# Start-up of a diffusion backbone step: products with constants from the start, four shifts on VectorE, a third chunk buffer, and the first normalized activations without GpSimd

## The chip, the core and the metric

The kernel runs on one core of a Trainium2 chip. The metric is the device time of one execution in microseconds (us); lower is better. TensorE (PE in the profile) multiplies matrices, VectorE (DVE) and ScalarE (ACT) do elementwise work, GpSimd (POOL) does slower elementwise work, and SyncE (SP) issues nearly all DMA transfers. Each engine executes its own instructions strictly in the order in which the program lists them, and waits on semaphores for the others.

## The reference

One inference step of a two-layer backbone over 384 tokens (256 latent and 128 context), model width 1024. The start of the program, which the change touches, is this part:

```
sh1, sc1, gt1, sh2, sc2, gt2 = split(silu(c) @ w_mod[l] + b_mod[l], 6)   # for c and for c_ctx
h = rmsnorm(x, norm_g[l, 0]) * (1 + sc1) + sh1                           # c for latents, c_ctx for context
z = h @ w_in_even                                                        # 1024 -> 3584
...                                                                      # attention, retention, output projection
x = x + gt1 * rmsnorm(m, norm_g[l, 1])
h = rmsnorm(x, norm_g[l, 2]) * (1 + sc2) + sh2
x = x + gt2 * rmsnorm(swiglu(h), norm_g[l, 3])
```

w_mod of a layer has 6144 columns, so 24 MB; the modulation of both layers is 48 MB of weights for two vectors c. Layer 0 has neighbourhood attention and retention (the even layer), layer 1 an HGRN2 mixer.

## The kernel before, in words

Everything is transposed: the model width lies on the 128 partitions in eight blocks (KT = 8, index j or k), tokens lie along the free axis (NT = 384). Every large product is made of three f32r products: activations are split into a high part `hh` and a low part `hl`, weights into `wh` (ScalarE) and `wl` (VectorE), and hh*wh + hh*wl + hl*wh is accumulated. A weight tile is 128 x 1024, eight blocks, 512 KB; three raw buffers `wr` and three pairs of split buffers rotate.

The modulation weights come in 48 chunks of 1 MB, in the order of MOD_ORDER. A chunk holds two blocks of 128 columns, for layer 0's first norm shift j and scale j (MOD_CHUNKS). "pe" chunks are multiplied by TensorE (`mod_pe`, eight products of 256 columns, then `mod_pe_out`: a ScalarE copy to `mev` and two small products with `sel` that add the four partial sums and turn them), "dve" chunks by VectorE (`mod_dve`, four multiply-and-accumulate instructions into `mscr`, against c spread over all partitions in `msb`). `mod_finish` adds the bias and makes the scale (1 + sc) * g. Two buffers `mraw` hold chunks.

The first norm (class `Norm`) doesn't wait for the root mean square. Of the first product group E1 (six output blocks, 8 x 6 x 3 = 144 matmuls), k goes over the blocks as they arrive: `early_hi` makes x[k] * scale on ScalarE and appends the two columns of shifts (386 columns), `early_lo` makes the low part on VectorE. The 1/rms row rB comes later and is applied when the six results leave. The other groups (E2, E5: 72 matmuls of 512 columns each, tokens as the stationary side; E3, E4, E6) use the truly normalized h, which `normed` makes per block: t = x * rB on GpSimd, hh = A t + S on ScalarE, the same once more into f on VectorE, hl = f - hh on VectorE. Attention starts with products of ka and qa, two of E1's results.

The order of the instructions is written by a planner (`Machine`): generators yield operations, and at each step the one with the earliest start by the planner's own costs is emitted, ties by priority. Its constants (COLD, the DMA rate in `Build.dma`) set the order on all engines and no more. load_mods interleaves chunk i with x[i]; load_weights the weight tiles; `rest` (line 1626) starts the loads of layer 0's other constants and `mod_dve`.

Of the kernel before, what the change touches and what calls it, by code (L numbers as in the profile page):

```python
# [36 lines left out]
P = 128  # L37
D = 1024
KT = 8
# [38 lines left out]
CB_AT = 4  # L78
# [21 lines left out]
COLD = 16.0  # L100
# [115 lines left out]
class Build:  # L216
# [71 lines left out]
    def dma(self, out, in_):  # L288
# [3 lines left out]
                  [a for a in here if a is in_], n / 355e3)  # L292
# [54 lines left out]
MOD_ORDER = ([("pe", 0, c) for c in range(8)]  # L347
# [9 lines left out]
def pack_mod(w):  # L357
# [120 lines left out]
def emit_all(nc, tc, ctx, io, outs):  # L478
# [24 lines left out]
    acc, rB = sb(cp, "acc", [NT]), sb(cp, "rB", [NT])  # L503
    acc2, rsd = sb(cp, "acc2", [NT]), sb(cp, "rsd", [96])
# [44 lines left out]
    start.loads = 0  # L549

    def load_mods():
        for i, (kind, l, ci) in enumerate(MOD_ORDER):
            r, = yield from mraw.take()
            yield I.dma(r, io["w_mod"][i])
            (mods.pe if kind == "pe" else mods.dve).append((l, ci, r))
            if i < KT:
                yield I.dma(x[:, i], io["xT"][:, i])
                start.loads = i + 1

# [17 lines left out]
    def mod_pe():  # L577

        for l, *chunks in MOD_PE:
# [15 lines left out]
            M.spawn(mod_pe_out(l, chunks, b), -1, margin=M_MOD)  # L595
# [12 lines left out]

    def mod_late():
# [7 lines left out]
    def mod_dve(phase, b):  # L617

        yield lambda: W.used >= DVE_FROM
        yield I.dma(b.sb, io["cB"])  # L620
        yield lambda: phase == 0 or len(W.norm.hs) == KT
        yield I.act(b.sb, b.sb, AF.Silu)
# [18 lines left out]
    mods.n, mods.over, mods.flying, mods.now = 0, set(), 0, False  # L641

# [152 lines left out]
    class Norm:  # L795


        def __init__(self, l, which):
# [9 lines left out]
            for par in range(2):  # L808
                M.spawn(self.normed(par), 2)

        def loads(self):
            for j in range(KT):
                yield lambda: start.loads > j
# [31 lines left out]
        def early_hi(self):  # L845
            for j in range(KT):
                yield lambda: self.x > j and (self.l, 12 * self.which + j) in mods.done
                for who, a, e in HALVES:
                    yield I.act(hh[:, j, a:e], x[:, j, a:e], AF.Identity, scale=self.coef(j, who)[0])
                yield I.act(hh[:, j, NT:NX], mod[self.l][:, 24 * self.which + j])  # L850
# [866 lines left out]
```

## Time and profile before

| | |
|---|---|
| median of 3 runs | 1129.93 us (1129.28 to 1131.42) |
| the profiled execution | 1129.32 us, its span 1127.5 us |
| PE busy | 1088.1 us (97% of the span) |
| DVE busy | 819.9 us (73%) |
| ACT busy | 541.8 us (48%) |
| POOL busy | 136.7 us (12%) |
| first product on PE | 6.87 us |
| first product of E1 | 13.32 us |
| first product of E2 | 52.40 us |
| first product of the first FFN-side output group after the retention norm | 211.94 us |

The profile is one execution. In the timeline a row gives the start, the duration, the engine, the source line, the operation with its output and inputs, how many instructions were merged, and in brackets how long the engine had sat idle before it and on what. Busy times of PE are modelled: consecutive matmuls overlap in the record, so the distance between two starts, not the duration, is what one costs.

### The profile page before, as it was taken

The numbers are of one execution on the slowest core, as the hardware profiler recorded it, in microseconds if no ns is written. First come the engines' busy times: TensorE is split into PE (matmuls) and PEld (weight loads), VectorE is DVE, ScalarE is ACT, GpSimd is POOL, SyncE is SP. The second block draws the span as 40 slices with busy tenths as digits, with TensorE's granted clock in tenths as the row PEclk, the third lists the DMA queues.
The fourth block names the chain that finished last, engine by engine and source line by source line (L and its number), as shares of the span: only waits on it lengthen the run. The fifth ranks groups of instructions, "written<-read, shape, count | busy, mean of one in ns | idle before, by whom it ended". The sixth has DMA issues, their size and how long they took to land.

```text
span 1127.5 us, 18541 instructions
## 1 busy us (share of the span) xinstructions
PE 1088.1 (97%) x7180; PEld 1011.7 (90%) x7180; DVE 819.9 (73%) x1524; ACT 541.8 (48%) x1002; POOL 136.7 (12%) x143
## 2 busy tenths in 40 slices
PE   6999999899999999999999999999999999999996
PEld 5778888679999999999887988888989999999995
DVE  2598888687989999995888489996786444444334
ACT  3585555368333333323765456655666333333321
POOL 1220000000000000234024046352000000000001
PEclk9999999999999999999999999999999999999998
DMA  9966544534667677565341322223224333333431
GB/s 351 359 215 215 168 149 132 215 136 152 233 241 240 238 245 240 205 227 167 135 156 62 127 85 85 76 76 103 94 84 141 122 123 129 123 123 129 131 112 56
DMA packets 49688, 180.44 MB, mean 160 GB/s; under 512 B 6560, under 2 KB 13728, under 8 KB 43072
## 3 DMA queue, kind: packets, MB, share of 16 engines
q1 hardware_dynamic: 49536, 179.18, 46.7%
q8 instruction: 56, 0.92, 0.3%
q14 instruction: 32, 0.26, 0.1%
q0 software_dynamic: 64, 0.08, 0.0%
HBM read 174.79 MB, written 3.41 MB: 158 GB/s over the span
## 4 chain that ended last, share of the span: by engine, by line
PE 77%; DVE 15%; issue 3%; DMA 2%; ACT 1%; SPq 1%; POOL 0%; DVEq 0%; ACTq 0%; POOLq 0%
PE bank L226 76%; DVE wl L252 3%; DVE mscr L265 2%; DMA mraw<-in_w_mod 2%; DVE XB L252 1%; DVE XA L252 1%; SPq L291 1%; DVE TA L252 1%; DVE scr L258 1%; PE bank L230 1%; DVE scr L252 1%; DMA ro<-qk 0%; DVE ZW L252 0%; DVE ac L282 0%; POOL ZW L250 0%
## 5 line engine op out<-in xcount | busy, mean ns | idle before, releaser
L226 PE MATMUL bank<-hh,wh 128*128 128x384 f32 (+1 forms) x1248 | 431.0, 345 | 0.0
L226 PE MATMUL bank<-hh,wl 128*128 128x384 f32 (+1 forms) x1248 | 425.4, 341 | 0.0
L226 PE MATMUL bank<-hl,wh 128*128 128x384 f32 (+1 forms) x1248 | 391.0, 344 | 0.0
L252 DVE TENSOR_TENSOR wl<-wr,wh 128x1024 fp32r<-128x1024 f32 x216 | 272.5, 1262 | 128.2 <-ACT wh L244 128.0
L244 ACT ACTIVATE wh<-wr 128x1024 fp32r<-128x1024 f32 x216 | 228.1, 1057 | 151.2 <-PE bank L226 106.0
L226 PEld LDWEIGHTS bank<-hh,wh 128*128 128x128 f32 x1248 | 237.9, 191 | 6.4 <-ACT scr L244 2.4
L226 PEld LDWEIGHTS bank<-hh,wl 128*128 128x128 f32 x1248 | 237.5, 190 | 0.9 <-issue 0.3
L226 PEld LDWEIGHTS bank<-hl,wh 128*128 128x128 f32 x1248 | 232.4, 189 | 5.6 <-issue 2.0
L265 DVE SCALAR_TENSOR_TENSOR mscr<-mraw,msb 128x1024 bf16<-128x1024 f32 x128 | 159.4, 1245 | 3.5 <-ACT msb L244 2.4
L226 PE MATMUL bank<-gh,wl 128*128 128x384 f32 x352 | 118.2, 336 | 1.8 <-DVE wl L252 1.8
L226 PE MATMUL bank<-gh,wh 128*128 128x384 f32 x352 | 117.6, 334 | 0.0
L226 PE MATMUL bank<-gl,wh 128*128 128x384 f32 x352 | 117.6, 334 | 0.0
L226 PEld LDWEIGHTS bank<-gh,wl 128*128 128x128 f32 x352 | 66.1, 188 | 3.4 <-DVE wl L252 3.4
L226 PEld LDWEIGHTS bank<-gl,wh 128*128 128x128 f32 x352 | 66.1, 188 | 0.0
L226 PEld LDWEIGHTS bank<-gh,wh 128*128 128x128 f32 x352 | 66.1, 188 | 0.0
L244 ACT ACTIVATE fs<-bank 128x384 f32<-128x384 f32 x44 | 21.1, 492 | 90.2 <-PE bank L226 90.2
L252 DVE TENSOR_TENSOR fs<-bank,fs 128x384 f32<-128x384 f32 x44 | 24.1, 556 | 39.4 <-PE bank L226 39.4
L244 ACT ACTIVATE gh<-fs 128x384 fp32r<-128x384 f32 x44 | 22.5, 519 | 57.7 <-DVE fs L252 57.6
L244 ACT ACTIVATE scr<-bank 128x384 f32<-128x384 f32 x44 | 21.9, 499 | 58.2 <-PE bank L226 58.2
L250 POOL TENSOR_TENSOR rB<-x,fy 128x384 f32<-128x384 f32 x1 | 1.9, 1877 | 387.3 <-DVE fy L258 387.3
L250 POOL TENSOR_TENSOR x<-x,fy 128x384 f32<-128x384 f32 x4 | 4.5, 1152 | 346.4 <-DVE fy L252 346.4
L250 POOL TENSOR_TENSOR ZW<-XB,TA 128x192 f32<-128x192 f32 x48 | 37.9, 810 | 31.8 <-ACT XA L244 17.4
(249 smaller groups left out, 1330.1 us busy)
## 6 DMA issues: line engine op xcount, KB each, us to landing
mraw<-in_w_mod SPq DMA_DIRECT2D x48, 1024.0 KB, 5.7
wr<-in_w_ffn_in SPq DMA_DIRECT2D x88, 512.0 KB, 3.3
wr<-in_w_ffn_out SPq DMA_DIRECT2D x44, 512.0 KB, 3.3
wr<-in_w_in_odd SPq DMA_DIRECT2D x40, 512.0 KB, 3.3
wr<-in_w_in_even SPq DMA_DIRECT2D x28, 512.0 KB, 4.4
wr<-in_w_out_even SPq DMA_DIRECT2D x8, 512.0 KB, 4.0
wr<-in_w_out_odd SPq DMA_DIRECT2D x8, 512.0 KB, 3.3
bias<-in_bias SPq DMA_DIRECT2D x8, 384.0 KB, 3.8
```

The source lines that it names most:

```text
L226: return Op("PE", lambda: self.nc.tensor.matmul(out, lhsT=lhsT, rhs=rhs, start=start, stop=stop), [out], [lhsT, rhs], cost + 0.004)
L230: return Op("PE", lambda: self.nc.tensor.transpose(out, in_, ident), [out], [in_], 0.11)
L244: return Op("ACT", lambda: self.nc.scalar.activation(out, in_, func, **kw), outs, ins, 0.1 + width(in_) / 1200, table)
L250: return Op("POOL", lambda: self.nc.gpsimd.tensor_tensor(out=out, in0=a, in1=b, op=op), [out], [a, b], 0.12 + n * 0.0021)
L252: return Op("DVE", lambda: self.nc.vector.tensor_tensor(out=out, in0=a, in1=b, op=op), [out], [a, b], 0.06 + n / 960)
L258: return Op("DVE", lambda: self.nc.vector.tensor_scalar(out=out, in0=a, scalar1=s1, scalar2=s2, op0=op0, **kw), [out], ins, 0.19 + width(o ...
L265: return Op("DVE", lambda: self.nc.vector.scalar_tensor_tensor(out=out, in0=a, scalar=s, in1=b, op0=op0, op1=op1, **kw), outs, ins, 0.1 + ...
L291: return Op("SP", lambda: self.nc.sync.dma_start(out, in_), [a for a in here if a is out], [a for a in here if a is in_], n / 355e3)
```

## The change

- Ten groups of four products of a constant tile of ones (40 instructions) stand at the start of TensorE's queue.
- For chunks 3 to 6 of the first eight (MIXED) the scale half stays on TensorE (eight products of 128 columns, `mod_scale`), and the shift half is computed on VectorE (`mod_shift`, two multiply-and-accumulate instructions of 1024 elements).
- For that c is needed on all partitions early: `spread_c` makes two diagonal tiles on VectorE, four TensorE products of 512 columns with ones, and four ScalarE copies into `msb`. The later load of c and its Silu are dropped for layer 0.
- x is loaded two blocks at a time; a third chunk buffer lies in the space of `cse` until `cse` itself is loaded; `rest` waits until the four shifts are done and the third buffer is given back.
- The small first loads are issued by ScalarE instead of SyncE; the identity matrix is loaded first and the rest of its tile after the fifth chunk.
- In `normed` t = x * rB moves from GpSimd to VectorE, and f from VectorE to ScalarE. Its priority is lower until `early_lo` is through.
- The planner's COLD goes from 16 to 7, its DMA rate from 355 to 400 bytes per ns.

```diff
-COLD = 16.0
+COLD = 7.0
...
-                  [a for a in here if a is in_], n / 355e3)
+                  [a for a in here if a is in_], n / 400e3)
...
+MIXED = (3, 4, 5, 6)
+MOD_ORDER = ([("mix" if c in MIXED else "pe", 0, c) for c in range(8)]
...
             r, = yield from mraw.take()
+            if r is start.third and i >= KT:
+                start.third = None
+                r, = yield from mraw.take()
             yield I.dma(r, io["w_mod"][i])
...
             if i < KT:
-                yield I.dma(x[:, i], io["xT"][:, i])
+                for j in range(nx, min(2 * i + 1, KT)):
+                    yield I.dma(x[:, j], io["xT"][:, j])
+                    start.x = nx = j + 1
                 start.loads = i + 1
+
+    def spread_c():
+
+        dg = [t.rearrange("p a b -> p (a b)")[:, :1024] for t in (L0.va, L0.vb)]
+        for who in range(2):
+            yield I.tt(dg[who].rearrange("p (k f) -> p k f", k=KT), ident.unsqueeze(1).to_broadcast([P, KT, P]),
+                       sc[:, :, who:who + 1].to_broadcast([P, KT, P]), MUL)
+        yield lambda: mods.n > 1 and norms[0].el > 0
+        for who in range(2):
+            for i in range(2):
+                b, = yield from banks.take()
+                yield I.mm(b, acc2[:, :P], dg[who][:, 512 * i:512 * i + 512])
+                yield I.act(L0.mod.sb[:, who, 512 * i:512 * i + 512], b)
+                banks.give(b)
+        mods.cb = True
...
+                if mixed:
+                    M.spawn(mod_shift(l, chunks[0], r), -1)
+                    rk = r[:, :1024].rearrange("p (k c) -> p k c", k=KT)
+                    for k0 in (0, 4):
+                        yield tuple(I.mm(b[32 * g:32 * g + 32, :P], sc[:, k0 + g], rk[:, k0 + g], k0 == 0, k0 == 4)
+                                    for g in range(4))
+                    break
...
+    def mod_shift(l, ci, r):
+        yield lambda: mods.cb
+        a, f = L0.mod.acc[ci % 2], MOD_CHUNKS[ci][0]
+        for who in range(2):
+            yield I.stt(L0.mod.scr, r[:, 1024:], 1.0, L0.mod.sb[:, who], MUL, MUL, a[:, 0, who:who + 1])
+        mraw.give(r)
+        yield I.ts(mod[l][:, f], a[:, 0], bmod[:, l, f:f + 1], ADD)
...
-                M.spawn(self.normed(par), 2)
+                M.spawn(self.normed(par), lambda: 2 if self.el == KT else 7)
...
-                yield I.tt(t, x[:, j], rB, MUL, pool=True)
+                yield I.tt(t, x[:, j], rB, MUL)
                 f, = yield from scr.take()
-                for who, a, e in HALVES:
-                    A, S = self.coef(j, who)
-                    yield I.act(hh[:, j, a:e], t[:, a:e], AF.Identity, bias=S, scale=A)
-                    yield I.ts(f[:, a:e], t[:, a:e], A, MUL, S, ADD)
+                for o in (hh[:, j, :NT], f):
+                    for who, a, e in HALVES:
+                        A, S = self.coef(j, who)
+                        yield I.act(o[:, a:e], t[:, a:e], AF.Identity, bias=S, scale=A)
...
-    nc.sync.dma_start(cT, io["cT"])
-    nc.sync.dma_start(ca, io["ca"])
+    nc.scalar.dma_start(cT, io["cT"])
+    nc.scalar.dma_start(ca, io["ca"])
+    nc.scalar.dma_start(ident, io["cb"][:, B_ID:B_ID + P])
...
+    for _ in range(FIRST):
+        for g in range(4):
+            M.emit(I.mm(o[32 * g:32 * g + 32, :P], acc2[:, :32], acc2[:, :P]))
...
-            yield lambda: W.used >= LOADS
+            yield lambda: W.used >= LOADS and mods.shifted == len(MIXED) and start.third is None
```

The planner turns this into other orders. Three places matter. The first is TensorE's queue at the very start (`acc` the tile of ones, `mraw` and `cse` the chunk buffers, `va` and `vb` the diagonal tiles of c, `ca` the constant with `sel`, `hh` with `wh` the first products of E1). Before:

```order
L226 MATMUL bank_63<-mraw_104,sc 32x256 x8
L226 MATMUL bank_63<-ca,mev 128x2 x2
L226 MATMUL bank_65<-mraw_105,sc 32x256 x8
L226 MATMUL bank_66<-hh,wh_110 128x386
L226 MATMUL bank_66<-hh,wl_113 128x386
```

And now:

```order
L227 MATMUL bank_70<-acc_87 32x128 x40
L227 MATMUL bank_63<-mraw_105,sc 32x256 x8
L227 MATMUL bank_63<-ca,mev 128x2 x2
L227 MATMUL bank_65<-mraw_106,sc 32x256 x8
L227 MATMUL bank_65<-ca,mev 128x2 x2
L227 MATMUL bank_65<-va,acc_87 128x512 x2
L227 MATMUL bank_66<-cse,sc 32x256 x8
L227 MATMUL bank_65<-vb,acc_87 128x512
L227 MATMUL bank_64<-scr_91,ca 32x96 x4
L227 MATMUL bank_66<-ca,mev 128x2 x2
L227 MATMUL bank_67<-hh,wh_111 128x386
```

E1 now begins behind the third chunk and three of the four products that spread c, no longer behind the second chunk.

The second is ScalarE's queue around the last early block of E1 (`hh<-x`, `hh<-mod`; `hh<-scr` is normalized h, `scr<-scr` the new f). Before, the last early block stood ahead of all normalized h:

```order
L244 ACTIVATE hh<-x,mod_80 128x256
L244 ACTIVATE hh<-x,mod_80 128x128
L244 ACTIVATE hh<-mod_80 128x2
L244 ACTIVATE wh_110<-wr_107 128x1024
L244 ACTIVATE rB<-bank_64 128x384
L244 ACTIVATE wh_111<-wr_108 128x1024
L244 ACTIVATE hh<-scr_93,mod_80 128x256
```

And now, from the row behind the eviction of the last of the eight chunks:

```order
L245 ACTIVATE wh_113<-wr_110 128x1024
L245 ACTIVATE hh<-scr_94,mod_80 128x256
L245 ACTIVATE hh<-scr_94,mod_80 128x128
L245 ACTIVATE scr_96<-scr_94,mod_80 128x256
L245 ACTIVATE scr_96<-scr_94,mod_80 128x128
L245 ACTIVATE hh<-scr_91,mod_80 128x256
L245 ACTIVATE hh<-scr_91,mod_80 128x128
L245 ACTIVATE scr_92<-scr_91,mod_80 128x256
L245 ACTIVATE scr_92<-scr_91,mod_80 128x128
L245 ACTIVATE hh<-scr_93,mod_80 128x256
L245 ACTIVATE hh<-scr_93,mod_80 128x128
L245 ACTIVATE hh<-x,mod_80 128x256
```

Two and a half normalized blocks now stand between the eviction of the last chunk and the last early block.

The third is VectorE's queue at the end of the retention (`ro`, `at`, `kd` the last head pair's operands, `mscr` the modulation on VectorE, `rs` and `scr` the retention norm). Before:

```order
L252 TENSOR_TENSOR at_159<-bank_63,scr_90 128x256 x2
L252 TENSOR_TENSOR kd_156<-bank_70,scr_92 128x128
L265 SCALAR_TENSOR_TENSOR mscr_132,macc_134<-mraw_105,msb_131 128x1024
L252 TENSOR_TENSOR kd_156<-bank_63,scr_90 128x128
L265 SCALAR_TENSOR_TENSOR mscr_132,macc_134<-mraw_105,msb_131 128x1024
L252 TENSOR_TENSOR mod_80<-macc_134,bmod 128x2x2
L265 SCALAR_TENSOR_TENSOR mod_80<-mod_80,gn 128x2
L252 TENSOR_TENSOR wl_115<-wr_109,wh_112 128x1024
L275 RECIPROCAL rs_88<-rs_88 128x96
```

And now:

```order
L253 TENSOR_TENSOR wl_115<-wr_109,wh_112 128x1024
L253 TENSOR_TENSOR wl_116<-wr_110,wh_113 128x1024
L253 TENSOR_TENSOR mod_80<-bank_66,bmod 128x2x4
L266 SCALAR_TENSOR_TENSOR mod_80<-mod_80,gn 128x4
L253 TENSOR_TENSOR ro_202<-bank_64,scr_93 128x256 x2
L253 TENSOR_TENSOR at_204<-bank_66,scr_94 128x256 x2
L253 TENSOR_TENSOR kd_201<-bank_64,scr_93 128x128
L253 TENSOR_TENSOR kd_201<-bank_66,scr_94 128x128
L276 RECIPROCAL rs_89<-rs_89 128x96
```

The last two modulation instructions have moved ahead of the retention's last pair, and so have, on TensorE, the two chunk products that stood inside the retention norm. Likewise, on VectorE, the first pair's `qd` had twelve instructions between it and the rotated `qk` that it needs, and now has one. From the FFN of layer 0 on, the order on TensorE is the same but for a few rows.

More of the change, by code (lines that the diff above doesn't have):

```diff
@@ L584, in mod_pe @@
             b, = yield from banks.take(1, 0 if mods.n < 8 or W.few else 2)
+            mixed = l == 0 and chunks[0] in MIXED
             for i in range(len(chunks)):
@@ L607, in mod_pe_out, with mod_scale @@
         mods.flying -= 1
+    def mod_scale(l, ci, b):
+        e, = yield from mev.take()
+        yield I.act(e[:, :P], b[:, :P])
+        yield I.mm(b[:, 0:2], e[:, :P], sel)
+        mev.give(e)
+        f, j = MOD_CHUNKS[ci][1], MOD_CHUNKS[ci][0] % KT
+        yield I.ts(mod[l][:, f], b[:, 0:2], bone[:, j:j + 1], ADD, gn[:, l, 2 * (ci // 12), j:j + 1], MUL)
+        banks.give(b)
+        mods.flying -= 1
+        mods.scaled.add((l, ci))
+    def mod_shift(l, ci, r):
[5 more added lines that the diff above has]
+        yield I.ts(mod[l][:, f], a[:, 0], bmod[:, l, f:f + 1], ADD)
+        yield lambda: (l, ci) in mods.scaled
+        mods.done.add((l, ci))
+        mods.shifted += 1
     def mod_late():
@@ L617, in mod_dve @@
     def mod_dve(phase, b):
[L619 to L622, printed above, removed]
+        yield lambda: W.used >= DVE_FROM and mods.shifted == len(MIXED)
+        if phase > 0:
+            yield I.dma(b.sb, io["cB"])
+            yield lambda: len(W.norm.hs) == KT
+            yield I.act(b.sb, b.sb, AF.Silu)
         for n in range(MOD_DVE[phase]):
@@ L808, in __init__ @@
             for par in range(2):
-                M.spawn(self.normed(par), 2)
+                M.spawn(self.normed(par), lambda: 2 if self.el == KT else 7)
         def loads(self):
             for j in range(KT):
-                yield lambda: start.loads > j
+                yield lambda: start.x > j
                 self.x = j + 1
@@ L846, in early_hi @@
             for j in range(KT):
-                yield lambda: self.x > j and (self.l, 12 * self.which + j) in mods.done
+                c = self.l, 12 * self.which + j
+                yield lambda: self.x > j and (c in mods.done or c in mods.scaled)
                 for who, a, e in HALVES:
                     yield I.act(hh[:, j, a:e], x[:, j, a:e], AF.Identity, scale=self.coef(j, who)[0])
+                yield lambda: c in mods.done
                 yield I.act(hh[:, j, NT:NX], mod[self.l][:, 24 * self.which + j])
@@ L1611, in emit_all @@
     nc.gpsimd.dma_start(gn, io["norm_g"])
+    o = banks.q[-1]
+    for _ in range(FIRST):
+        for g in range(4):
+            M.emit(I.mm(o[32 * g:32 * g + 32, :P], acc2[:, :32], acc2[:, :P]))
+    M.emit(I.ts(bone, bmod[:, 0, KT:2 * KT], 1.0, ADD))
     def load_cb():
-        yield lambda: start.loads >= CB_AT
-        yield I.dma(cb, io["cb"])
+        yield lambda: start.loads >= C_AT
+        yield I.dma(cb[:, B_BC:], io["cb"][:, B_BC:])
     M.spawn(load_cb(), 1)
@@ L1622, in emit_all @@
         open_l0(lp)
+        M.spawn(spread_c(), 1)
+        start.third = L0.cse[:, :2048]
+        mraw.give(start.third)
         norms[0] = Norm(0, 0)
```

18 lines of the change are left out of this document (13 added, 5 removed).

## Prediction

> **What bounds the kernel now.** I read the windows first, to see where TensorE loses time, then the timeline at the places found, then the groups by shape for prices. PE is busy for 97% of the span, so only its gaps and its half-speed stretches can be won. The windows (columns: PE, PEld, DVE, ACT, POOL busy, clock, DMA share, GB/s) are cut at 3.4 us:
>
> ```profile
> 5.90:9.30 3.40, 1.94 (x16) 0.68 (x16) 0.00 (x0) 0.91 (x2) 0.00 (x0) 1.00 1.00 392
> 12.70:16.10 3.40, 3.40 (x18) 2.78 (x11) 1.68 (x4) 1.73 (x3) 1.01 (x1) 1.00 0.99 401
> 53.50:56.90 3.40, 1.77 (x6) 1.16 (x7) 3.40 (x7) 1.49 (x4) 1.13 (x1) 0.98 1.02 384
> 56.90:60.30 3.40, 3.40 (x10) 2.65 (x9) 3.40 (x7) 2.68 (x7) 2.04 (x2) 0.51 0.55 215
> 207.10:210.50 3.40, 1.66 (x18) 0.72 (x18) 2.33 (x4) 0.00 (x0) 0.00 (x0) 0.98 1.02 431
> 210.50:213.90 3.40, 3.40 (x15) 2.24 (x8) 1.72 (x4) 1.12 (x2) 0.00 (x0) 0.51 1.02 419
> ```
>
> Twice a window in which PE was busy for about half (1.77 and 1.66 of 3.40) is followed by one at clock 0.51. The first 16 us read 1.00, but the timeline shows half speed there too:
>
> ```profile
> 1.65 0.43 SPq L291 DMA_DIRECT2D mraw<-in_w_mod  x1
> 6.87 1.94 PE L226 MATMUL bank<-mraw,sc 128*32 128x256 f32 x16 [6.87 <-DMA mraw<-in_w_mod]
> 13.32 0.69 PE L226 MATMUL bank<-hh,wh 128*128 128x386 f32 x1
> 14.13 0.53 PE L226 MATMUL bank<-hh,wh 128*128 128x386 f32 x1
> 14.45 0.53 PE L226 MATMUL bank<-hh,wl 128*128 128x386 f32 x1
> 19.71 0.34 PE L226 MATMUL bank<-hh,wh 128*128 128x386 f32 x1
> 19.89 0.34 PE L226 MATMUL bank<-hh,wl 128*128 128x386 f32 x1
> 22.88 1.07 PE L226 MATMUL bank<-mraw,sc 128*32 128x256 f32 x16
> 52.40 0.39 PE L226 MATMUL bank<-wh,hh 128*128 128x512 f32 x1
> 52.63 0.39 PE L226 MATMUL bank<-wl,hh 128*128 128x512 f32 x1
> 54.88 0.50 PE L226 MATMUL bank<-wh,hl 128*128 128x512 f32 x1 [1.86 <-DVE hl L252]
> 69.25 0.79 ACT L244 ACTIVATE qa<-qa,wb 128x256 f32<-128x256 f32 x2
> 71.14 1.78 PE L226 MATMUL bank<-ka,qa 64*128 64x384 f32 x12
> 72.85 0.50 PE L226 MATMUL bank<-wh,hh 128*128 128x512 f32 x1
> 137.78 0.34 PE L226 MATMUL bank<-hh,wl 128*128 128x384 f32 x1
> 137.41 1.22 DVE L252 TENSOR_TENSOR wl<-wr,wh 128x1024 fp32r<-128x1024 f32 x1
> 139.08 0.68 DVE L252 TENSOR_TENSOR qd<-qd,qk 128x512 f32<-128x512 f32 x1
> 139.82 1.13 PE L226 MATMUL bank<-qd,s 128*128 128x256 f32 x4 [1.70 <-DVE qd L252]
> 208.45 0.91 PE L226 MATMUL bank<-scr,cse 128*128 128x384 f32 x2 [2.66 <-DVE scr L252]
> 209.76 1.38 PE L226 MATMUL bank<-mraw,sc 128*32 128x256 f32 x16 [0.39 <-DMA mraw<-in_w_mod]
> ```
>
> A chunk product costs 1.94 us early and 1.07 later, an E1 matmul 0.32 us from start to start (14.13 to 14.45) and then 0.18 (19.71 to 19.89). E1 runs from 13.32 to about 52.3. E2 then waits for normalized h (54.88) and falls to half clock. Its 72 matmuls and six score products end at about 76.3: 15 matmuls are left at 72.85, at 0.23 each (52.40 to 52.63). Later there are a wait of 1.70 at 139.82 and one of 2.66 at the end of the retention.
>
> The prices come from the groups by shape of the first 75 us (instructions, then busy us and mean ns) and, for mscr, from the page:
>
> ```profile
> L252 DVE TENSOR_TENSOR wl<-wr,wh 128x1024 fp32r<-128x1024 f32 x11 | 13.4, 1221 | 19.1 <-ACT wh L244 19.1
> L244 ACT ACTIVATE wh<-wr 128x1024 fp32r<-128x1024 f32 x12 | 12.5, 1048 | 0.8 <-DMA wr<-in_w_in_even 0.7
> L250 POOL TENSOR_TENSOR scr<-x,rB 128x384 f32<-128x384 f32 x8 | 9.7, 1216 | 11.3 <-ACT rB L244 4.8 <-DVE hl L252 4.2 <-ACT ka L244 1.1
> L258 DVE TENSOR_SCALAR scr<-scr,mod 128x256 f32<-128x256 f32 x8 | 5.8, 741 | 0.9 <-POOL scr L250 0.9
> L258 DVE TENSOR_SCALAR scr<-scr,mod 128x128 f32<-128x128 f32 x8 | 4.0, 513 | 0.0
> L244 ACT ACTIVATE hh<-scr,mod 128x256 fp32r<-128x256 f32 x8 | 4.8, 595 | 0.8 <-POOL scr L250 0.7
> L244 ACT ACTIVATE hh<-scr,mod 128x128 fp32r<-128x128 f32 x8 | 3.7, 480 | 0.0
> L244 ACT ACTIVATE hh<-x,mod 128x256 fp32r<-128x256 f32 x8 | 4.1, 510 | 14.2 <-DVE mod L265 14.2
> L244 ACT ACTIVATE mev<-bank 128x256 f32<-128x256 f32 x8 | 3.0, 380 | 3.9 <-PE bank L226 3.8
> L244 ACT ACTIVATE ka<-scr,wb 128x256 f32<-128x256 f32 x4 | 2.0, 510 | 3.6 <-DVE wb L269 3.6
> L244 ACT ACTIVATE ka<-scr,wb 128x128 f32<-128x128 f32 x4 | 1.6, 388 | 0.0
> L226 PE MATMUL bank<-rs,cb 128*128 128x96 f32 x8 | 1.0, 271 | 0.0
> L252 DVE TENSOR_TENSOR scr<-bank,rB 128x384 f32<-128x384 f32 x4 | 2.2, 542 | 0.0
> L265 DVE SCALAR_TENSOR_TENSOR mscr<-mraw,msb 128x1024 bf16<-128x1024 f32 x128 | 159.4, 1245 | 3.5 <-ACT msb L244 2.4
> ```
>
> **The start.** With the two small loads off SyncE, the first chunk is issued 0.9 us earlier (1.65 to about 0.75); 64 KB of identity go beside it, so it lands at about 6.1 instead of 6.87. The 40 constant products are half as wide as a chunk product's: 16 records took 1.94 cold, so 40 of half the width take about 40 x 0.12 = 4.8 us, from 1.0 to 5.8. They delay nothing, and the first chunk should meet full speed. What then arrives is set by DMA at 0.39 to 0.40 MB/us (392 and 401 GB/s in the windows): x0, a weight tile and the second chunk, 1.77 MB, take 4.5 us, to 10.6; x1, x2, a tile and the third chunk, 1.97 MB, 5.0 us, to 15.6. x in pairs puts 0.5 us ahead of that chunk; the third buffer costs nothing here.
>
> In the new order E1 stands behind the third chunk's product. Ahead of that stand two products that spread c through one bank, so that the second waits for a ScalarE copy, itself behind a weight split and a block of h. Counting through: second chunk's product to 11.9, its scale and shift at 14.0, first spread product to 14.75, copy to 15.95, second to 16.95, third chunk to 18.2, the third spread product, the squares and the small products to 19.75. **E1 begins at about 19.8, against 13.32.** A spread product of 512 columns is priced between 0.8 and 1.1 us (four 96-column products took 1.02 for 384 columns); I take 0.85, since they run from start to start in less than their busy time.
>
> What PE then has left at full speed is 144 x 0.175 = 25.2 us of E1, four half products at 1.0 with their small products, a whole one at 1.6, a spread product 0.85, squares 0.3 and the spread of 1/rms 0.8: 32.8 us, dense to 52.6. VectorE has eight more mscr of 1.245 here, 10.0 us. It was busy for 1.68 of 3.40 us in the window at 12.7, and 10.0 over 33 us of E1 add 1.0 to that, so I let them hide behind PE; if E1 waited for each of them, they would cost all 10.0.
>
> Is PE still at full speed? Between 7.1 and 10.6 it has only 0.4 us of work, less than the 1.77 and 1.66 after which it went to 0.51. So I count one window at half clock, which falls mostly into waits for DMA and moves the spread by 0.4 us: E1 from 20.2 to 53.0. A second window would make it 1.4. The Trainium skill (TensorE: Matmul & The Clock Gate, section "What's actually happening") gives the cold state as following at least one idle window of about 3.4 us. By that rule the gap of 3.1 us here, and the half-busy windows above, would leave the clock up; the two rows at 0.51 say otherwise. By the rule the sum is 0.4 us less, by the rows as given.
>
> **From E1 to E2.** t on VectorE costs 0.54 instead of 1.22 on GpSimd; f leaves VectorE (0.74 + 0.51 = 1.25 a block) and costs ScalarE a pair like hh's, 0.595 + 0.48 = 1.08, or like ka's, 0.51 + 0.39 = 0.90. I take 1.0, between them. VectorE, full in the window at 53.5, gets 10.0 - 4.3 = 5.7 us back. But ScalarE must now do, from the eviction of the eighth chunk (at 43.7: PE reaches that chunk 22.3 us after E1's start, and evicts 1.2 later) to the second qa: the eviction 0.4, five wh 5.2, sixteen pairs 16.0, the last early block 1.1 (0.51, and less for its two smaller pieces), four ka pairs 3.2 to 3.6, two qa pairs 1.6 to 1.8. That is 27.7 us, without a gap, to 71.4; before, qa was ready at 70.04. E1's last block stands behind two and a half normalized blocks in that queue, so E1 ends 1.9 us late, near 55, and PE waits; E2's first four blocks are then ready, so the wait of 1.86 at 54.88 goes. PE does the score products from 71.5 to 73.2, and 21 matmuls instead of 15 remain, 4.85 us: **E2 ends at 78.1 against 76.3, 1.8 later.** The wait has moved from VectorE to ScalarE. With f at 0.90 it is 0.8 less; with two cold windows 1.0 more.
>
> **Later.** c needn't be loaded and put through Silu again, and two of the 32 mscr that remain for layer 0 are done earlier. At 139.82 the qd that PE awaits no longer stands behind a split and an attention step (137.41 to 139.08), only behind one mscr: 1.7 us go, or nothing if PE comes there later by itself. At the retention's end one mscr (1.2) leaves the way from at to the second kd, a product (1.07) leaves the norm's chain, and so do 0.39 of waiting for a chunk; the wait of 2.66 for sqrt, reciprocal and a product stays, with its half clock behind it. As PE has to do these products earlier, I count 1.8, between 0.4 and 2.7. After 214 us the order hardly differs, and I count nothing.
>
> **Sum**, against the profiled 1129.32 us (the median of before is 1129.93): +1.8 at E2's end, -1.7, -1.8, so -1.7: **1127.6 us.**
>
> **The rivals.** *The early order holds (1123.9).* E1 is dense from 18.2 (the third chunk's landing at 15.6, its product, the small ones), so the eighth chunk is evicted at 41.7; with f at 0.90 qa is ready at 68.6 and E2 ends at 75.2, 1.1 earlier than before. With 1.7 and the upper 2.7 won later that is 5.5. For it speaks VectorE's relief, against it ScalarE's queue, which leaves no more than this even then.
> *ScalarE's queue carries its lateness through (1132.8).* If qa is ready at 73.5, 3.5 late, because f costs 1.08 and E1's last block is late too, attention starts late on a VectorE that is busy for 3.40 of 3.40 even now, and nothing is regained before 205. This decides from a qa later than 72.5.
> *The change doesn't do what it says (1130.3).* Narrow products of ones don't raise the clock. Then the first two chunk products cost 0.87 more each (1.94 against 1.07), the small ones about 0.5 each, and all 2.7 reach qa.
>
> **How the numbers follow.** Under 0.2% (2.3 us) a measurement can't tell the kernels apart. The forecast has 0.45 and spreads by 2 us either way, so half of it is within 0.2%: faster 0.23, same 0.22. The better order has 0.22, all faster. The late queue has 0.22, slower 0.20, same 0.02. The missing warmth has 0.11, same 0.08, slower 0.03. Together: faster 0.45, same 0.32, slower 0.23. The range of 8 in 10 reaches to both outer cases, and 2 us below the better one for the order between 78 and 205 that I have not costed: 1121.5 to 1133; the likeliest case alone is 1125.6 to 1129.6.
>
> **What would show it.** Right: a first chunk product of 1.07 us at about 6.1, E1's first product near 20, a row at 0.51 before 17, PE waiting for `hl<-x` shortly before E1 ends, ScalarE without gaps from 44 to 71, score products near 71.5, and no wait for qd near 138. Wrong: E1 starting before 17 or ending before 51, qa before 69 (then the better order), or after 73 with a wait still at qd (then the late queue); a first product of 1.94 us says that the constants didn't warm the clock.

## The result, and the profile after

The changed kernel takes 1143.89 us (median; 1143.21 to 1144.07) against 1129.61 for before on the same chip: a ratio of 1.0123, 95% interval 1.0108 to 1.0139. It is slower, by 1.2% or 14 us; the forecast was 1127.6, within 1121.5 to 1133. The profiled execution took 1143.21 us, its span 1141.4 (before: 1129.32 and 1127.5).

Where the 14 us come from is told by the weight matmuls: both kernels have 5,088 of them (`hh,wh`, `hh,wl`, `hl,wh` and the like), in the same sequence, so the start of one in one trace minus its start in the other is the lag at that point of the work. A place is named by the number of weight matmuls ahead of it. The lag can be read only where TensorE has done the same other products in both kernels, and the places of the table are such (but for the products of the start, which the change itself adds or moves).

| weight matmuls ahead | what starts there | before, us | changed, us | lag |
|---|---|---|---|---|
| 0 | E1 | 13.3 | 25.2 | +11.9 |
| 144 | E2 | 52.4 | 59.2 | +6.8 |
| 216 | end of E2 | 76.4 | 79.7 | +3.3 |
| 373 | | 118.5 | 122.0 | +3.5 |
| 449 | behind the first `qd` | 140.6 | 142.1 | +1.5 |
| 520 | third retention pair next | 162.1 | 163.5 | +1.4 |
| 612 | | 189.6 | 195.3 | +5.7 |
| 648 | | 195.9 | 201.7 | +5.7 |
| 684 | behind the retention norm | 216.5 | 229.0 | +12.6 |
| 960 | FFN of layer 0 | 278.7 | 292.3 | +13.6 |
| 5,087 | the last one | 1114.7 | 1128.6 | +13.9 |

The start is 11.9 us late. At E2's end 3.3 us are left, and they stay until 139 us, where before waited 1.70 us for `qd` and the changed kernel doesn't; 1.5 are left behind that. The rest of the loss is made in two stretches, from 164 to 195 us and from 202 to 229. (At places with unlike work the lag misleads: at 432 it reads -0.3, but there the changed kernel has still to do an attention group, which before did at 126.24 and it does at 134.86, and which takes some 3.5 us.) Here is TensorE's start in the timeline of the changed kernel, with its entry into E2, the score products and the first product with `qd`:

```profile
1.06 4.50 PE L227 MATMUL bank<-acc 128*32 128x128 f32 x80 [1.06 <-DVE acc L1666]
6.41 1.93 PE L227 MATMUL bank<-mraw,sc 128*32 128x256 f32 x16 [0.86 <-ACT sc L1673]
10.78 1.93 PE L227 MATMUL bank<-mraw,sc 128*32 128x256 f32 x16 [0.91 <-DMA mraw<-in_w_mod]
16.03 2.08 PE L227 MATMUL bank<-va,acc 128*128 128x512 f32 x2 [0.33 <-DVE mod L253]
18.79 2.07 PE L227 MATMUL bank<-va,acc 128*128 128x512 f32 x2 [0.69 <-ACT msb L245]
20.80 1.94 PE L227 MATMUL bank<-cse,sc 128*32 128x256 f32 x16
22.66 1.81 PE L227 MATMUL bank<-vb,acc 128*128 128x512 f32 x2
25.18 0.42 PE L227 MATMUL bank<-hh,wh 128*128 128x386 f32 x1
59.15 0.40 PE L227 MATMUL bank<-wh,hh 128*128 128x512 f32 x1
73.05 1.78 PE L227 MATMUL bank<-ka,qa 64*128 64x384 f32 x12 [0.35 <-ACT qa L245]
139.12 1.02 PE L227 MATMUL bank<-qd,s 128*128 128x256 f32 x4
```

All three chunk products are cold here (1.93, 1.93, 1.94), a spread product takes 2.08 instead of the 0.85 forecast, and E1 begins at 25.18. From there PE is dense up to E2. The retention's end, TensorE and then VectorE:

```profile
182.19 0.48 PE L227 MATMUL bank<-qk 64*128 64x128 f32 x2 [1.56 <-DVE ro L253]
183.99 0.48 PE L227 MATMUL bank<-qk 64*128 64x128 f32 x2 [1.31 <-DVE at L253]
205.95 1.07 PE L227 MATMUL bank<-mraw,sc 128*32 128x256 f32 x16
208.09 1.07 PE L227 MATMUL bank<-mraw,sc 128*32 128x256 f32 x16 [1.07 <-DMA mraw<-in_w_mod]
209.88 1.05 PE L227 MATMUL bank<-ca,mev 128*128 128x2 f32 x8 [0.72 <-ACT mev L245]
210.86 3.60 PE L227 MATMUL bank<-qk 64*128 64x256 f32 x12
217.96 0.55 PE L227 MATMUL bank<-scr,cse 128*32 128x96 f32 x8 [1.17 <-ACT scr L245]
221.00 2.93 PE L227 MATMUL bank<-scr,cse 128*128 128x384 f32 x4 [2.48 <-DVE scr L253]
```

```profile
180.78 0.69 DVE L253 TENSOR_TENSOR ro<-ro,cse 128x512 f32<-128x512 f32 x1 [3.22 <-DMA ro<-qk]
181.39 0.75 DVE L253 TENSOR_TENSOR ro<-bank,scr 128x256 f32<-128x256 f32 x2
182.05 0.42 DVE L253 TENSOR_TENSOR at<-bank,scr 128x256 f32<-128x256 f32 x1
182.38 1.22 DVE L253 TENSOR_TENSOR wl<-wr,wh 128x1024 fp32r<-128x1024 f32 x1
183.51 0.42 DVE L253 TENSOR_TENSOR at<-bank,scr 128x256 f32<-128x256 f32 x1
```

The same places in before, VectorE's wait for the rotation, TensorE's for the third pair's results, and the last pair's score products:

```profile
178.07 0.69 DVE L252 TENSOR_TENSOR ro<-ro,cse 128x512 f32<-128x512 f32 x1 [2.31 <-DMA ro<-qk]
181.42 0.48 PE L226 MATMUL bank<-qk 64*128 64x128 f32 x2 [0.37 <-DVE ro L252]
198.13 1.13 PE L226 MATMUL bank<-qk 64*128 64x256 f32 x8
```

Two things are to be seen. At 180.78 VectorE waits 3.22 us for the transfer that rotates the last pair (`ro<-ro,cse`), and the third pair's results (`ro<-bank`, `at<-bank`), which TensorE wants at 180.6, stand behind that wait; one of them also behind a weight split. In before VectorE waited there too, but only until 178.07, and TensorE waited 0.37 us. And the last pair's score products (`qk` at 210.86) stand behind both remaining modulation products, with no weight matmul left to run meanwhile; in before they stood at 198.13, with weight matmuls behind them. Now scores, decay, attention products, root mean square and its spread follow each other from 210.86 to 224.4, most of them waiting for the one before. The windows (columns as in the prediction) show what the waits do to the clock:

```profile
180.30:183.70 3.40, 0.82 (x4) 0.30 (x3) 2.92 (x6) 1.44 (x2) 0.00 (x0) 1.00 0.07 19
183.70:187.10 3.40, 3.11 (x12) 1.58 (x12) 3.02 (x8) 0.00 (x0) 0.00 (x0) 0.62 0.46 154
207.10:210.50 3.40, 1.69 (x22) 1.04 (x22) 1.23 (x1) 0.61 (x2) 0.00 (x0) 1.00 1.05 340
210.50:213.90 3.40, 3.34 (x15) 2.18 (x16) 2.03 (x7) 0.00 (x0) 0.00 (x0) 0.69 0.89 364
213.90:217.30 3.40, 2.89 (x14) 1.51 (x14) 0.40 (x2) 0.43 (x1) 0.00 (x0) 0.50 0.94 395
217.30:220.70 3.40, 0.55 (x8) 0.20 (x8) 1.07 (x2) 2.20 (x4) 0.00 (x0) 0.50 0.01 2
220.70:224.10 3.40, 2.93 (x4) 1.18 (x4) 1.35 (x3) 0.24 (x1) 0.00 (x0) 0.50 0.01 2
```

In before this stretch had one window at half clock (0.51 at 210.5); now every window from 213.9 to 227.5 reads 0.50.

### The profile page after: what moved, and what is told of

It is laid out like the page before. It is cut to its first block, busy times and chain, and to the rows that moved or that the text cites. A ratio compares the mean times of both kernels' runs of the same rounds, so it can differ in the third digit from the quotient of the medians.

```text
span 1141.4 us, 18698 instructions
## 1 busy us (share of the span) xinstructions
PE 1101.1 (96%) x7260; PEld 1019.1 (89%) x7260; DVE 831.5 (73%) x1536; ACT 546.2 (48%) x1020; POOL 127.9 (11%) x135
## 5 line engine op out<-in xcount | busy, mean ns | idle before, releaser
L266 DVE SCALAR_TENSOR_TENSOR mscr<-mraw,msb 128x1024 bf16<-128x1024 f32 x134 | 168.0, 1254 | 5.7 <-DMA wr<-in_w_ffn_in 4.4
L227 PE MATMUL bank<-wh,hh 128*128 128x512 f32 x96 | 40.4, 421 | 0.3 <-DVE wb L270 0.3
```

The lines of the kernel that those rows point to most:

```text
L227: return Op("PE", lambda: self.nc.tensor.matmul(out, lhsT=lhsT, rhs=rhs, start=start, stop=stop), [out], [lhsT, rhs], cost + 0.004)
L266: return Op("DVE", lambda: self.nc.vector.scalar_tensor_tensor(out=out, in0=a, scalar=s, in1=b, op0=op0, op1=op1, **kw), outs, ins, 0.1 + ...
```

## The experiments

**Theory O**: the 14 us are lost by the order that the planner now writes for the retention's end. **Rival S**: the late start, or the work that it adds to VectorE and ScalarE, carries through in whatever order. In most of these kernels the planner follows a list, operation by operation, of the picks that it made for another of the kernels; so the order of one stage can be exchanged, or one instruction moved, with all else kept. The start that kernels with one order share still differs by about 1 us between profiled executions. The lags against before of the runs used most, in us:

| matmuls ahead | changed | 1: changed, then before's order | 2: before, then changed order | 8: before's order from E2's end | 5: bank later | 6: rotation later | 7: both | 9: 7 and ones | 10: 7 and split | 11: all |
|---|---|---|---|---|---|---|---|---|---|---|
| 0 | +11.9 | +12.2 | 0.0 | +11.8 | +11.1 | +12.2 | +11.5 | +9.6 | +11.6 | +8.9 |
| 216 | +3.3 | +3.6 | -0.5 | +3.2 | +2.5 | +3.7 | +3.0 | +1.1 | +3.0 | +0.3 |
| 373 | +3.5 | +3.8 | -0.5 | +3.3 | +2.7 | +3.9 | +3.2 | +1.3 | +3.2 | +0.5 |
| 520 | +1.4 | +2.7 | +0.6 | +1.7 | +0.5 | +1.8 | +1.0 | -0.9 | +1.1 | -1.6 |
| 612 | +5.7 | +4.0 | +6.2 | +2.6 | +6.2 | +3.0 | +3.7 | +0.4 | +1.2 | -1.6 |
| 684 | +12.6 | +3.5 | +12.9 | +2.1 | +3.1 | +9.6 | +0.7 | -2.7 | -1.9 | -4.6 |
| 960 | +13.6 | +4.5 | +13.1 | +3.2 | +3.1 | +11.0 | +0.6 | -1.5 | -0.7 | -4.8 |
| time, us | 1143.89 | 1134.13 | 1144.68 | 1133.48 | 1134.01 | 1140.13 | 1130.68 | 1128.31 | 1129.78 | 1126.08 |

### The start or the order (1, 2, 8)

```diff
+    M.follow = lambda: W.used >= 22
...
+            if self.follow():
+                s = self.listed()
+                if s is not None and s.head is not None:
+                    best = s
             ops, best.head = best.head, None
```

Experiment 1 is the changed kernel up to its 22nd weight tile and then before's order:

> The changed kernel's own order up to its 22nd weight tile (528 weight matmuls, about 163 us), from there the order of before, operation by operation. Theory O (the 14 us are lost by the order at the retention's end: VectorE's wait for the rotation's transfer at 180.78, and the last pair's score products behind the 672nd matmul and behind both modulation products): the lag at the 540th matmul was 0.1 us, so 1129 to 1131 us, the 576th weight matmul within 1 us of before's 177.5, the 684th within 2 us of 216.5. Rival S (the start's lateness or VectorE's added work carries through whatever the order): 1140 to 1145 us, with waits of PE for VectorE between 175 and 230.

Experiment 2 is the reverse:

> The reverse: before up to its 22nd weight tile, from there the changed kernel's order; the start is before's (E1 at 13.3). Theory O: the loss of 177 to 229 comes with the order, so 1138 to 1144 us, the 684th weight matmul near 226 to 229. Rival S: 1128 to 1131 us, the 684th near 216.5.

Experiment 8 takes before's order from the 10th tile on:

> The changed kernel's own order up to the end of E2 (10 weight tiles, 80 us, where it is 3.3 us late), from there the order of before. Theory O: before's waits between 80 and 140 us (1.70 for qd at 139.82 among them) take up part of the 3.3, and nothing is lost at 177 to 229: 1129 to 1133 us. Rival S (the start's work itself costs it): 1138 us or more.

Measured: 1134.13 us (ratio to before 1.0038, 1.0026 to 1.0050), 1144.68 (1.0130, 1.0112 to 1.0148) and 1133.48 (1.0035, 1.0017 to 1.0054). Experiment 2 has before's start, with E1 at 13.3 us, and still loses everything, by the same waits:

```profile
181.77 0.48 PE L255 MATMUL bank<-qk 64*128 64x128 f32 x2 [1.83 <-DVE ro L281]
183.56 0.79 PE L255 MATMUL bank<-qk 64*128 64x128 f32 x2 [1.31 <-DVE at L281]
211.25 1.53 PE L255 MATMUL bank<-qk 64*128 64x256 f32 x8
221.21 2.93 PE L255 MATMUL bank<-scr,cse 128*128 128x384 f32 x4 [2.48 <-DVE scr L281]
```

So the order is enough to lose 14 us, and the changed start with before's order loses 3.5 to 4, 10 less. Rival S is out as the main cause. The sizes of theory O were missed. Experiment 1 was expected at 1129 to 1131, from a lag of 0.1 at the 540th matmul; but there the changed kernel had score products of 1.1 us still to do, and the lag was 1.4 just before. It grew to 2.7 where the two orders join and to 4.0 by 612. In experiment 8, half a microsecond above its range, PE waits 0.28 us for `qd` instead of 1.70, and the lag falls from 3.3 to 1.7 there: before's wait takes up a part of the lateness, as expected. The rest stays, between 1.7 and 3.5 us.

### The small loads and the constants (3, 4)

Three loads back on SyncE, and no constants (`FIRST = 0`):

```diff
-    nc.scalar.dma_start(cT, io["cT"])
-    nc.scalar.dma_start(ca, io["ca"])
-    nc.scalar.dma_start(ident, io["cb"][:, B_ID:B_ID + P])
+    nc.sync.dma_start(cT, io["cT"])
+    nc.sync.dma_start(ca, io["ca"])
+    nc.sync.dma_start(ident, io["cb"][:, B_ID:B_ID + P])
```

> The changed kernel with its three small first loads (c, ca, the identity) issued by SyncE ahead of the chunks instead of by ScalarE; the order on all other engines is the same, row by row. c then lands near 2.7 us as in before instead of 6.1, the identity near 4 instead of 9.3, the first chunk 0.9 to 1.4 later. Both theories: E1 begins 1 to 3 us earlier than 25.2. Theory O: what the start wins is taken up by the waits before 134 us, so within 1.5 us of the changed kernel, 1142.5 to 1145.5. Rival S: the whole gain of the start arrives, 1140.5 to 1142.5.

> The changed kernel without the 40 constant products; the order is otherwise the same row by row. If the products of 32 columns didn't raise the clock: the first chunk product still takes 1.93 us at about 6.4, E1 begins within 0.5 us of 25.2, and the time is within 1 us of the changed kernel's 1143.9. If they did hold the clock up somewhere: E1 begins 1 to 2 us later, and by theory O the time is still within 1.5 us, by rival S 1 to 2 us more.

Measured: 1143.76 us (1143.23 to 1144.04) and 1144.15 (1142.72 to 1144.72); neither differs from the changed kernel. With SyncE's loads the second chunk product starts at 13.11 instead of 10.78, and E1 begins at 25.18, as in the changed kernel: the 1 to 3 us expected didn't come, and the test of theory O that lay in them fell away. Without the constants E1 begins at 25.55. As they stand the constants are worth nothing. The profiled execution of the changed kernel was one in which they didn't warm the clock, but that made no difference: in experiments 1, 5, 6 and 7, with the same start and a first chunk product of 1.07, E1 begins at 24.4 to 25.6.

### The two places (5, 6, 7)

The modulation product of chunks 16 and 17 takes its PSUM bank when three are free and keeps it while it waits for the second chunk; the last pair's scores need two. Experiment 5 lets it take the bank only when the last pair is through:

```diff
         for l, *chunks in MOD_PE:
+            yield lambda: chunks[0] != 16 or ("ob", 3) in ev
```

> The changed kernel, but the product of chunks 16 and 17 takes its PSUM bank only once the last retention pair is through; the order is otherwise the changed kernel's. So the last pair's score products stand at the 662nd weight matmul (before: 660th) instead of behind the 672nd and behind 16 modulation products, which now fill the norm's waits. Theory O: most of the 6.8 us that the lag grows between the 648th and the 684th weight matmul goes, 5 to 7 us, so 1137 to 1139.5 us. Rival (the chunks' transfers or the half clock set this stretch, not the place of the products): less than 2 us, 1142 to 1144.5.

Experiment 6 moves one instruction on VectorE:

```diff
 TENSOR_TENSOR scr<-scr,cb 128x128
-TENSOR_TENSOR ro<-ro,cse 128x512
 TENSOR_TENSOR ro<-bank,scr 128x256 x2
...
 TENSOR_TENSOR kd<-bank,scr 128x128
+TENSOR_TENSOR ro<-ro,cse 128x512
 TENSOR_TENSOR qk<-qk,cse 128x2x256
```

> The changed kernel with one instruction moved: on VectorE the last pair's product of the rotated copy (ro<-ro,cse, which waited 3.22 us for its transfer at 180.78) stands behind the third pair's six products instead of ahead of them. Theory O: PE's waits of 1.56 (ro) and 1.31 (at) go, and with them some 1.5 us at half clock behind them: the lag at the 612th weight matmul falls from 5.7 to between 1 and 3, the time to 1139 to 1141 us. Rival (the rotation's transfer is late anyhow and the wait only moves on to the last pair): within 1 us of 1143.9.

> Both edits together: chunks 16 and 17 take their bank after the last pair, and the rotation's product stands behind the third pair's. Theory O: the two add up, 8 to 12 us, 1132 to 1136 us. Rival (the same lateness is met twice, so the one's gain is a part of the other's): no better than the better of the two alone by more than 1 us, about 1137 to 1139.

Measured: 1134.01 us, 1140.13, and both together 1130.68 (ratio to before 1.0010, 1.0000 to 1.0020). That is 9.9, 3.8 and 13.2 less than the changed kernel: the two add up to nearly the whole loss. Experiment 6 came out as expected, 5 and 7 gained more than expected. The timeline and a window of experiment 5:

```profile
204.68 1.14 PE L256 MATMUL bank<-qk 64*128 64x256 f32 x8
210.10 1.50 PE L256 MATMUL bank<-mraw,sc 128*32 128x256 f32 x24
214.36 1.54 PE L256 MATMUL bank<-scr,cse 128*128 128x384 f32 x4
```

```profile
213.90:217.30 3.40, 2.25 (x11) 1.37 (x11) 2.10 (x6) 0.52 (x1) 0.00 (x0) 1.00 0.99 377
```

The scores now run at 204.68 among weight matmuls, the modulation products fill the norm's waits, the clock reads 1.00 where it read 0.50, and the spread is at 214.36 instead of 221.00. From 648 to 684 the lag falls by 3.1 us where it grew by 6.8. That this is more than the 5 to 7 expected we put down to the half clock, which went with the waits, before's own window at 210.5 included; no run separates the two. Experiment 6 took away the wait for `ro`; that for `at`, behind the weight split, stayed at 1.31.

### What is left at this place, and at the start (9, 10, 11)

In experiment 7 PE has hardly a gap between E1's start and 180 us. So experiment 9 adds products of ones behind the first two chunk products, where PE idled:

```diff
+FILL = 8
...
+                    more = FILL if l == 0 and chunks[0] < 2 and k0 == 4 else 0
...
+                                + [I.mm(banks.q[-1][32 * g:32 * g + 32, :P], acc2[:, :32], acc2[:, :P])
+                                   for _ in range(more) for g in range(4)])
```

> The kernel with both edits of the retention's end (1130.7 us), and 32 further products of ones behind the first and behind the second chunk product, to keep PE busy where it idled (8.9 to 11 and 13 to 14.8) and the clock up. Theory C (E1 begins at 24.9 instead of 20 because the clock falls again in these gaps; from E1 to 180 us PE has hardly a gap, so what the start wins arrives): second chunk product 1.07, the three spread products before E1 near 1.05 instead of 2.08, E1 from 21 to 22.5, the time 2 to 3.5 us less: 1127 to 1129. Rival (ScalarE's queue, full until qa, sets E2's end): E1 begins earlier, but qa stays near 72.5 and the time falls by less than 1 us.

Experiment 10 instead moves the weight split behind the third pair's `at`:

```diff
-TENSOR_TENSOR at<-bank,scr 128x256
+TENSOR_TENSOR at<-bank,scr 128x256 x2
 TENSOR_TENSOR wl<-wr,wh 128x1024
-TENSOR_TENSOR at<-bank,scr 128x256
```

> The kernel with both edits, and one more instruction moved: on VectorE the weight split that stood between the third pair's two products of at (wl<-wr,wh, 1.22 us) goes behind them. PE's wait of 1.31 us for at at 182.05 goes; if the half clock of the 3.4 us behind it (granted clock 0.50 from 183.8) comes from that wait, it goes too. Theory O: 1.3 + 1.7 = 3.0 us less, 1127 to 1128.5. Rival (the wait alone): 1.3 less, 1129.4; nothing, if PE then waits for the split's tile.

> All edits together: chunks 16 and 17 after the last pair, the rotation's product and the weight split behind the third pair's products, and the further products of ones at the start. Theories C and O: the gains add, 1124 to 1126.5 us, less than before by 0.3 to 0.5%. If C falls: as the run without the further ones, 1127 to 1129.5.

Measured: 1128.31 us, 1129.78, and with everything 1126.08, a ratio to before of 0.9976 (0.9961 to 0.9990): this one is faster than both kernels. In experiment 9's start the second chunk product and all three spread products are at full speed, and E1 begins at 22.9 (between them, from 12.6 to 16.0, one window still reads 0.50; in experiment 11 none does, and E1 begins at 22.2):

```profile
6.45 1.07 PE L257 MATMUL bank<-mraw,sc 128*32 128x256 f32 x16 [0.90 <-ACT sc L1708]
10.84 1.07 PE L257 MATMUL bank<-mraw,sc 128*32 128x256 f32 x16 [1.03 <-DMA mraw<-in_w_mod]
17.25 1.12 PE L257 MATMUL bank<-va,acc 128*128 128x512 f32 x2 [0.33 <-DVE mod L283]
```

The 1.9 us by which E1 starts earlier than in experiment 7 are 2.4 us in the time: theory C holds, and ScalarE's queue doesn't keep the gain. For experiment 10 the windows of 7 and then of 10 over the same stretch:

```profile
180.40:183.80 3.40, 2.09 (x14) 1.26 (x14) 2.94 (x7) 1.38 (x2) 0.00 (x0) 1.00 0.30 108
183.80:187.20 3.40, 3.40 (x13) 2.68 (x12) 3.40 (x7) 1.81 (x4) 0.00 (x0) 0.50 0.11 46
```

```profile
180.40:183.80 3.40, 3.22 (x21) 1.99 (x22) 3.40 (x8) 1.76 (x3) 0.00 (x0) 1.00 0.28 69
183.80:187.20 3.40, 3.40 (x26) 3.00 (x25) 3.40 (x7) 1.49 (x4) 0.00 (x0) 1.00 0.27 106
```

Without the wait PE is busy for 3.22 us instead of 2.09, and the half clock behind it is gone. Of the lag 2.5 us go here (+3.7 to +1.2 at the 612th matmul). The time is only 0.9 less, though, and missed the range of 1127 to 1128.5: in the profiled execution 1.2 us come back between the 720th and the 960th matmul, where the norm ahead of the FFN has one window more at half clock than in experiment 7. Whether the other executions have that window too is not shown.

### The wait for qd (12)

Before, with two instructions moved:

```diff
-        po, = yield from banks.take()
-        for d in range(2):
-            yield I.mm(po[:, :NS], s0[:, d], qd[:, d], d == 0, False)
+        if hp > 0:
+            po, = yield from banks.take()
+            for d in range(2):
+                yield I.mm(po[:, :NS], s0[:, d], qd[:, d], d == 0, False)
...
+        if hp == 0:
+            po, = yield from banks.take()
+            for d in range(2):
+                yield I.mm(po[:, :NS], s0[:, d], qd[:, d], d == 0, False)
```

> Before, with two PE instructions of the first retention pair (the product of qd with the state, which waits 1.70 us for qd at 139.82) moved 27 weight matmuls on, to just ahead of that pair's score products; all else in before's order. If the forecast's term for this wait was right: 1.7 us less, 1128 to 1128.5. Rival (the wait only moves on to the next result of VectorE): within 0.7 us of before's 1129.8.

Measured: 1131.17 us (ratio 1.0014, 1.0001 to 1.0026), 1.3 us above before's 1129.90 on the same chip, so outside both ranges. Nothing was won, and the mechanism is the rival's:

```profile
140.18 0.33 PE L259 MATMUL bank<-cb,as 128*128 128x128 f32 x1 [1.69 <-DVE as L287]
```

The wait is as long as before, 1.69 us, for the next of VectorE's results. VectorE was busy for 3.40 of 3.40 us from 138.0 there, so it was late as a whole; `qd` was only the first to show it.

### Which part of the change brings the order (13 to 16)

Experiment 13 is before with the part on normalized h alone, 14 the changed kernel without that part, 15 without the mixed chunks (`MIXED = ()`), 16 with the two old planner constants (`COLD = 16.0`, 355).

> Before with only the part on normed h (t on VectorE, f on ScalarE, its lower priority), order by the planner. The start is before's. In its new order the last pair's score products stand behind the 672nd weight matmul and behind the modulation product, as in the changed kernel. Theory O (the order of the retention's end decides, whatever part brings it): slower than before by 4 to 8 us, 1134 to 1138, although E2 ends no later. Rival N (the part itself counts: VectorE is relieved before E2): 1126 to 1130 us.

> The changed kernel with normed h made as before (t on GpSimd, f on VectorE), order by the planner: the start is the changed kernel's, but the last pair's score products stand at the 623rd weight matmul, so with 49 of them still to fill its waits. Theory O: no loss at 205 to 229, 1130 to 1137 us. Rival S (the start): 1141 to 1145 us.

> The changed kernel with no mixed chunks: all eight first chunks are multiplied whole by TensorE, no shifts on VectorE; constants, x in pairs, third buffer and normed h stay. In its order the last pair's scores stand at the 614th weight matmul. Theory O: 1129 to 1136 us. Rival (the shifts on VectorE were worth the change, and without them E1 is longer by their 4 us): 1140 us or more.

> The changed kernel with the planner's two old constants (16 and 355). The last pair's scores stay behind the 672nd matmul and the modulation products, the rest of the order moves. Theory O: the late scores cost 5 to 8 us again, 1136 to 1144 us. Rival (the two constants made the order worse): 1129 to 1133 us.

Measured: 1143.87 us (1.0109, 1.0084 to 1.0133), 1138.72 (1.0072, 1.0045 to 1.0099), 1131.17 (1.0014, 1.0000 to 1.0027) and 1148.36 (1.0159, 1.0143 to 1.0175). The two with the late place of the scores (13 and 16) lose most, the two with the early place (14 and 15) less, in the sense expected; the sizes were missed in three of four, only 15 lies in its range. From 373 to 684 the lag grows from 5.0 to 14.3 us in 13 and from 13.9 to 16.6 in 16; it goes from 5.6 to 5.9 in 14 and from 6.5 to 4.3 in 15 (where some modulation products, 1.5 and 1.0 us, are still to be done). Experiment 13 is the sharpest: before's start, one part of the change, and 13 us lost. Its timeline:

```profile
69.34 0.50 PE L226 MATMUL bank<-wh,hh 128*128 128x512 f32 x1 [3.52 <-ACT hh L244]
209.38 1.93 PE L226 MATMUL bank<-mraw,sc 128*32 128x256 f32 x16 [4.30 <-DMA mraw<-in_w_mod]
224.72 1.65 PE L226 MATMUL bank<-scr,cse 128*128 128x384 f32 x2 [2.48 <-DVE scr L252]
```

PE waits 3.52 us for ScalarE's hh in E2 (lag +4.1 at its end), 4.30 for the chunk, with the scores behind it, and goes through the norm's chain alone. Experiment 14 has its scores among the matmuls (205.60). The rotation still costs PE a wait there:

```profile
189.25 0.49 PE L227 MATMUL bank<-qk 64*128 64x128 f32 x2 [1.76 <-DVE ro L253]
```

But most of its loss lies elsewhere: 5.5 us of lag at E2's end, and another 5.0 between 720 and 960. Experiment 16 lost 14.0 us before E2's end already. So no one part is the trigger: with the part on normalized h alone the scores come late (13), and without that part or without the mixed chunks they come early (14, 15). We take it that each part shifts the planner's clock a little; why the planner comes to the late order in each case was not followed further.

## Why the prediction was wrong

**The step that failed is the last term, "at the retention's end ... I count 1.8".** It read the new order only from where `at` and `kd` go on to the norm: an mscr and a product leave that chain, so it gets shorter. The same rows said that the two chunk products now stand ahead of the last pair. The pair had thereby lost the weight matmuls that hid it, and its scores a bank. The place of the score products among the weight matmuls, which says so, is not in the prediction. Instead of -1.8 the stretch from the 648th to the 684th matmul cost +6.8, and 9.4 of lag go when the pair is put back (experiment 5). The wait of VectorE for the rotation (+4.3 from 520 to 612) was in no term: "the order between 78 and 205 that I have not costed" got 2 us of range, downward. Term by term, in us:

| stretch | forecast | measured, by the lag |
|---|---|---|
| to E2's end | +1.8 | +3.3 |
| the wait for `qd` (216 to 520) | -1.7 | -1.9 |
| the rotation (520 to 612) | no term | +4.3 |
| the retention's end (612 to 684) | -1.8 | +6.9 |
| behind it | 0 | +1.3 |
| sum | -1.7 | +13.9 |

**The start.** The first term, E1 at 20.2, was 5 us too early. The constants did raise the clock for the first product in most executions, but it fell again in the gap of 2 to 3 us behind it, and the three spread products ran cold, at 2.08, 2.07 and 1.81 where 0.85 was taken. The price at full speed is 1.12 (experiment 9), a little above the 0.8 to 1.1 given. One cold window had been counted; PE was cold until about 24 us. The first product didn't start with the chunk's landing but with c (`sc`), whose small load landed near 6.1.

**E1 to E2.** E1 took 34.0 us (25.2 to 59.2) against 32.8. ScalarE was full from the eviction of the eighth chunk to qa, as said; a pair cost 0.88 from start to start, not 1.0, which is 1.9 us over sixteen; with the other pieces, also shorter from start to start than the durations summed, it took 24.7 us instead of 27.7:

```profile
49.30 0.39 ACT L245 ACTIVATE mev<-bank 128x256 f32<-128x256 f32 x1 [1.74 <-PE bank L227]
50.53 0.97 ACT L245 ACTIVATE hh<-scr,mod 128x256 fp32r<-128x256 f32 x2
51.41 0.98 ACT L245 ACTIVATE scr<-scr,mod 128x256 f32<-128x256 f32 x2
72.50 1.48 ACT L245 ACTIVATE qa<-qa,wb 128x256 f32<-128x256 f32 x4
```

With E1 5 us later and the pairs cheaper, E2's end came 3.3 late, against 1.8. PE didn't wait for the last early block.

**The wait for qd** went, and 1.9 us of lag with it, near the 1.7 forecast. That is in part luck: the term rested on the new place of `qd` on VectorE, but in before's order too the wait shrinks to 0.28 when PE comes there 3.3 us late (experiment 8), and with PE on time moving the product wins nothing (experiment 12).

**The rivals.** The late queue was right up to E2's end: qa ready at 74.0 (it said 73.5), and 3.3 us late. But "nothing is regained before 205" was wrong: 1.9 us were, at the wait for `qd`. No rival looked for a loss behind that, in the stretch that the forecast counted as a gain. "The change doesn't do what it says" was half true: the constants warm the clock in most executions and then do nothing, since it cools again.

## What to carry to other kernels

Where a planner writes the order, a change at the start can cost most at the other end of its stage: before summing what shortens a chain, look up for each of its steps how many independent matmuls stand around it, before and after. A wait at the head of an in-order queue is paid by what stands behind it, so an instruction that waits for a slow transfer belongs behind the results that TensorE wants first. A wait is a price to be won only if what releases the next one isn't late as well. And two traces can be compared by the start of the same instruction only where the same work lies behind both.

## What the runs showed of the hardware

*Products of 32 columns of ones raise the clock, but not in every execution.* Of the thirteen profiled kernels that begin with 40 of them at 1.05 us, the first chunk product, at 6.4 to 7.4, took 1.07 us in ten and 1.93 in three; in the five that begin without, it took 1.93 or 1.94. The Trainium skill (TensorE: Matmul & The Clock Gate, section "What's actually happening") says that the window of the monitor runs free of the kernel's start; that would explain it. The traces agree as far as they go: the granted clock was 0.50 for 3.4 us at a time in before (from 210.4) and for 17.1, five times that, in the changed kernel (from 211.8). A gap of about 3.3 us with some 0.6 us of work in it behind that product was enough to be cold again at 11 us (experiment 7: 1.68 of 3.40 us busy from 6.3, then 0.50); 32 further products in it kept the clock up (experiment 9: 1.07 at 10.84).

*A window need not be idle to lower the clock.* PE was busy for 2.09 of 3.40 us at 180.4 in experiment 7, its longest gap 1.31, and 0.50 was granted next; at 3.22 (experiment 10) it stayed at 1.00. The same section of the Trainium skill has the cold state follow at least one idle window of about 3.4 us, which doesn't fit that. The busy share alone doesn't decide it either: in experiment 12 PE was busy for 1.71 us from 138.0 to 141.4, with a gap of 1.69, and the next window stayed at 1.00.

*A small load issued by ScalarE beside a 1 MB transfer was slow to land.* c was issued at 0.74, at the same time as SyncE's first chunk, landed 5.3 us later and was used at 6.14, behind a wait of 2.50 us for it. Issued by SyncE ahead of the chunk it landed after 1.8 us (before) and 1.6 (experiment 3):

```profile
0.74 0.41 ACTq L1669 DMA_DIRECT2D cT<-in_cT  x1
6.14 0.22 ACT L1673 ACTIVATE sc<-cT 128x16 f32<-128x16 f32 x1 [2.50 <-DMA cT<-in_cT]
```
